# A hybrid trunk layer: convolution taps paced behind weight splits, and RWKV's GroupNorm as a step of its own

## The chip, the cores and the metric

One Trainium2 chip, one of its cores. The metric is the device time of one execution of the program in microseconds (us); the time of a kernel is the median of its runs.

## What is computed

One layer of a decoder trunk on x of 1024 tokens x 1024 channels, all in float32. One input projection feeds three groups of heads, and one output projection joins them; a gated MLP with a short convolution and a last norm follow.

```python
h = rms_norm(x, norm_mix)
p_conv, p_nsa, p_rwkv = split(h @ w_in)
y_conv = silu(layer_norm(causal_dwconv(u * sigmoid(gate), width 31)))   # 256 channels
y_nsa  = gates . (compressed, selected, sliding-window attention)       # 8 heads of 64
y_rwkv = (layer_norm_per_head(delta_rule_scan(r, w, k, v, a)) + bonus) * g   # 4 heads of 64
x = x + concat(y_conv, y_nsa, y_rwkv) @ w_out
x = x + (silu(causal_dwconv(h2 @ w_gate, width 3)) * (h2 @ w_up)) @ w_down    # h2 = rms_norm(x)
out = rms_norm(x)
```

`layer_norm_per_head` is the "GroupNorm" of this document: each head's 64 values are centred and scaled by the root of their variance, for each token.

## The kernel before

The program has phases. **Phase 1** makes all projections of the normalised input (the projection matmuls are L229), the convolution, and most of the RWKV group. **Phase 2** is the attention, one tile of 128 tokens after another (queries times keys L897/L898, transposes L922, probabilities times values L930), with the rest of the RWKV group between. Then come the output projection (**phase o**: loads of the joined groups L988, matmuls L229 into bank rw) and the MLP.

A projection block (`proj_T`) loads a weight block of 1024 x 128 in two halves (`wload`). Each half is split (`split`, L118) into a high part, copied and rounded by ACT (whi, L120), and a low part, the difference, made by DVE (wlo, L121). Then 24 matmuls of 512 columns for each half of the tokens follow (`mm3`, L229: high x high, high x low, low x high). PE reads the split parts, so ACT and DVE must split in time. Weights have two buffers (wraw, whi, wlo).

The convolution of width 31 works on 256 channels, as two tiles of 128 channels x 1024 tokens. Tile 0 is done by DVE: 31 instructions ("taps", L270 and 30 times L272) that multiply and add in place on 128 x 1024. Tile 1 is shared out: ACT scales a copy (ctap, L278) and POOL adds it (L279), 60 times on 128 x 512, and ctap has two buffers, so ACT can be two ahead of POOL. When both tiles are done, a LayerNorm over the channels follows (L284 on; its squares are L289, its matmuls L294 and L303). Its output goes to the DRAM tensor md (L311).

The RWKV group is worked off in four units (j, h): j picks two heads, h half of the tokens. A unit has three steps. S (`rwkv_prep`, `rwkv_mats`) prepares and, on POOL, runs a recurrence of 62 small instructions (L532, L534); its inputs and outputs go through DRAM. V (`rwkv_solve`) solves triangular systems with small matmuls (L554 to L581). C (`rwkv_chain`) runs over 8 chunks, each reading the state H that the one before has left (L597 to L615), and fills the PSUM bank py. In C, right behind the chunks, stands the GroupNorm (L619 to L642): sums and squares (L621 to L629), an inverse root on DVE (`rsqrt`, L106 to L116), four transposes on PE (L635), ACT's scale and shift (L637), the bonus and the gate (L638 to L641, with matmul L640), and a store to md (L642).

The order is made in two stages. The string `steps` gives the order in which the program's steps are written; RWKV's steps S, V and C are written under a high priority. Then a scheduler at build time lists every engine's instructions from these priorities and its own model of times. Each engine works its list strictly in order: an instruction that waits holds all behind it. SP issues all DMAs from one list in the same way. So a change of the steps moves instructions on all engines, far from where it was written. `hT` are the normalised inputs, `KEY.ev` below is the pair that evacuates a key projection: ACT's copy L689 and DVE's difference L690.

Before, the steps read

```python
steps="lora r0 S00 conv taps V00 S01 keys q C00 V01 r1a cmp0 r1b cmp1 r1c S10 C01 V10 S11 C10 V11 C11"
```

where keys, q, r1a, r1b, r1c, cmp0 and cmp1 are projections (keys, queries, the second pair of RWKV heads, compressed keys and values).

## Time and profile before

| | |
|---|---|
| median of 3 runs | 1483.7 us (1480.32 to 1494.8) |
| the profiled execution: its own time | 1479.4 us |
| its span (first to last instruction) | 1477.5 us |
| PE busy | 1388.7 us (94%) |
| DVE, ACT, POOL busy | 1002.7 (68%), 686.9 (46%), 499.2 (34%) us |
| share of PE in the chain that ended last | 79% |

PE is the engine that sets the time. It is idle for 89 us of the span, and those 89 us are not spread evenly: they lie around 165 to 245 us, around 361 to 377 us, and around 704 to 726 us. So the profile is read by stretches, and within each by what PE waited for. The granted clock of PE (PEclk, a share of full speed; the two levels are 1.2 and 2.4 GHz, so 0.50 is a stretch wholly at the lower one) is read beside it, because it has fallen wherever PE has been idle.

### The profile page before, as it was taken

To read this page: it belongs to the slowest core of one execution; us is meant where nothing else is said; L and a number is where in the kernel's file an instruction comes from. 1 tells how busy PE (TensorE), PEld (TensorE's weight loads), DVE (VectorE), ACT (ScalarE), POOL (GpSimd) and SP (SyncE) were. 2 spreads that over 40 slices of the span, in tenths; PEclk is the share of its full clock that TensorE was granted. 3 is DMA by queue.
4 is the path that set the end of the run, shared out by engine and by line. 5 is a ranking of instruction groups with operands and counts; after the bars stand their busy time and mean duration, and the time that the engine had idled before them with its cause. 6 is when DMAs were issued, how large, how long until landed. Compare 5 with 4: busy or idle time off the path is not lost.

```text
span 1477.5 us, 22767 instructions
## 1 busy us (share of the span) xinstructions
PE 1388.7 (94%) x7897; PEld 1095.2 (74%) x7897; DVE 1002.7 (68%) x2187; ACT 686.9 (46%) x1377; POOL 499.2 (34%) x607
## 2 busy tenths in 40 slices
PE   6999589998899999999799899999999999999997
PEld 5887457776677676766588677888788788888886
DVE  6347594454868778798257867676775776666685
ACT  5441245624456665678223533343343333445463
POOL 1002996921144066220000144443444442113310
PEclk9999888999899999999899999999999999999999
DMA  6133133436514254542722123332332334986533
GB/s 185 40 107 82 44 103 111 142 84 179 153 33 139 78 154 125 181 150 81 240 89 83 43 93 93 108 107 70 104 113 93 108 100 162 388 280 216 188 92 114
DMA packets 206679, 186.69 MB, mean 126 GB/s; under 512 B 56355, under 2 KB 145764, under 8 KB 206564
## 3 DMA queue, kind: packets, MB, share of 16 engines
q1 hardware_dynamic: 206564, 185.24, 40.3%
q8 instruction: 62, 1.02, 0.3%
q14 instruction: 53, 0.43, 0.1%
HBM read 126.99 MB, written 58.20 MB: 125 GB/s over the span
## 4 chain that ended last, share of the span: by engine, by line
PE 79%; DVE 8%; POOL 4%; DMA 3%; ACT 2%; issue 2%; SPq 1%; ACTq 0%; DVEq 0%; POOLq 0%
PE gb L229 13%; PE mm L229 12%; PE rw L229 10%; PE ga L229 9%; PE gc L229 8%; PE tr L229 5%; PE tr L922 5%; PE av L930 4%; PE mm L897 2%; PE mm L898 2%; POOL sT L534 1%; POOL sx L532 1%; DVE pp L901 1%; POOL cacc L279 1%; DVE pp L915 1%
## 5 line engine op out<-in xcount | busy, mean ns | idle before, releaser
L229 PE MATMUL mm<-hT,whi 128*128 128x512 f32 x608 | 200.3, 409 | 19.6 <-DVE ev L690 14.8
L229 PEld LDWEIGHTS mm<-hT,whi 128*128 128x128 f32 x608 | 115.7, 193 | 48.9 <-ACT whi L120 20.2
L229 PE MATMUL mm<-hT,wlo 128*128 128x512 f32 x304 | 123.0, 407 | 1.9 <-DVE wlo L121 1.9
L925 ACT ACTIVATE pT<-tr 128x512 f32<-128x512 f32 (+1 forms) x152 | 79.9, 536 | 60.6 <-PE tr L922 59.2
L930 PE MATMUL av<-pT,V 128*64 128x128 f32 x1056 | 96.0, 287 | 1.5 <-ACT pT L925 1.5
L1076 POOL TENSOR_TENSOR S<-wraw,wr 128x512 f32<-128x512 f32 x22 | 28.5, 1296 | 192.8 <-DVE or L107 91.1
L922 PE MATMUL tr<-idn,pp 128*128 128x128 f32 x528 | 90.3, 289 | 1.8 <-DVE pp L915 1.8
L279 POOL TENSOR_TENSOR cacc<-cacc,ctap 128x512 f32<-128x512 f32 x60 | 85.1, 1429 | 12.7 <-ACT ctap L278 12.4
L121 DVE TENSOR_TENSOR sp<-rb,sp 128x512 fp32r<-128x512 f32 x66 | 55.6, 842 | 49.4 <-ACT sp L120 49.4
L229 PE MATMUL rw<-woh,mix 128*128 128x512 f32 x240 | 79.5, 407 | 9.0 <-ACT mix L120 9.0
L229 PE MATMUL rw<-sp,sp 128*128 128x512 f32 x330 | 86.0, 389 | 0.0
L229 PE MATMUL tr<-sp,sp 128*128 128x512 f32 x330 | 85.9, 389 | 0.0
L897 PE MATMUL mm<-KH,QS 128*128 128x512 f32 (+2 forms) x192 | 77.7, 411 | 3.1 <-DVE mx L901 2.8
L930 PEld LDWEIGHTS av<-pT,V 128*64 128x64 f32 x1056 | 59.2, 136 | 28.3 <-issue 13.7
L922 PEld LDWEIGHTS tr<-idn,pp 128*128 128x128 f32 x528 | 55.9, 141 | 30.5 <-issue 29.1
L915 DVE TENSOR_SCALAR pp<-pp,sm 128x640 f32<-128x640 f32 (+7 forms) x128 | 76.5, 638 | 0.9
L120 ACT ACTIVATE sp<-rb 128x512 fp32r<-128x512 f32 x66 | 41.6, 630 | 74.1 <-PE tr L229 36.5
L121 DVE TENSOR_TENSOR sp<-b,sp 128x512 fp32r<-128x512 f32 x88 | 72.1, 827 | 5.2 <-ACT sp L120 5.0
L229 PEld LDWEIGHTS mm<-hT,wlo 128*128 128x128 f32 x304 | 58.5, 193 | 18.1 <-DVE wlo L121 3.8
L229 PEld LDWEIGHTS tr<-sp,sp 128*128 128x128 f32 x330 | 61.9, 188 | 12.9
L229 PEld LDWEIGHTS rw<-sp,sp 128*128 128x128 f32 x330 | 61.9, 188 | 12.9
L532 POOL TENSOR_TENSOR sx<-sN,sT 128x60 f32<-128x60 f32 (+24 forms) x124 | 48.0, 387 | 63.0 <-DMA sN<-dn 54.9
(455 smaller groups left out, 3648.8 us busy)
## 6 DMA issues: line engine op xcount, KB each, us to landing
wr<-in_ffn_w_gate_dram SPq DMA_DIRECT2D x44, 256.0 KB
wraw<-in_ffn_w_up_dram SPq DMA_DIRECT2D x44, 256.0 KB
pdS<-prod SPq DMA_DIRECT2D x44, 256.0 KB
b<-pdS SPq DMA_DIRECT2D x44, 256.0 KB
rb<-tdT SPq DMA_DIRECT2D x44, 256.0 KB
pdA<-prod SPq DMA_DIRECT2D x33, 256.0 KB
b<-pdA SPq DMA_DIRECT2D x33, 256.0 KB
wraw<-in_w_in_dram SPq DMA_DIRECT2D x30, 256.0 KB
```

Of the source, the lines that this page charges most:

```text
L120: self.nc.scalar.activation(hi, src, AF.Copy)
L121: getattr(self.nc, eng).tensor_tensor(lo, src, hi.bitcast(F32), op=ALU.subtract)
L229: mm = lambda l, r, **k: self.nc.tensor.matmul(out, l, r, skip_group_check=more, **k)
L279: nc.gpsimd.tensor_tensor(t[:, o:o + 512], t[:, o:o + 512], z, op=ALU.add)
L532: v_.tensor_tensor(x, N[:, q, q + 1:32].unsqueeze(2).to_broadcast([P, n, w]), Tm[:, q, 0:w].unsqueeze(1).to_broadcast([P, n, w]), op=ALU.mult)
L897: pe.matmul(pts[g][:, 0:n], QS[:, r, g, :], KH[g][hf][:, ks], start=True, stop=False)
L898: pe.matmul(pts[g][:, 0:n], QS[:, r, g, :], KL[g][hf][:, ks], start=False, stop=True)
L915: v.tensor_scalar(Ps[g], Ps[g], sm[:, g:g + 1], None, op0=ALU.mult)
L922: pe.transpose(pt[:, o:o + P], Ps[g][:, kt * P:kt * P + P], self.idn)
L925: s.activation(pT[:, 0:n], pt[:, 0:n], AF.Copy)
L930: pe.matmul(av[g * 64:g * 64 + 64, r * P:r * P + P], self.V[kk // 2][:, kk % 2, vo + g * 64:vo + g * 64 + 64], pT[:, o:o + P], start=first ...
L1076: gp.tensor_tensor(t, x, y, op=op)
```

## The change

Two things. First, the convolution is cut in two steps. `taps` (`conv_taps`) now writes the part of ACT and POOL at once, and puts the 31 instructions of DVE in a list, `self.fill`; each split of a weight half in `wload` then issues two of them (`pace=2`) behind itself. What is left, and the LayerNorm, is the new step `cend` (`conv_rest`), behind cmp0. Second, the GroupNorm is cut out of `rwkv_chain` and becomes `rwkv_norm`, a step N under the same high priority, that stands behind the next unit's solve (N11 behind C11). The work of every instruction stays what it was.

```diff
-steps="lora r0 S00 conv taps V00 S01 keys q C00 V01 r1a cmp0 r1b cmp1 r1c S10 C01 V10 S11 C10 V11 C11"
+steps="lora r0 S00 conv taps V00 S01 keys q C00 V01 N00 r1a cmp0 cend r1b cmp1 r1c S10 C01 V10 N01 S11 C10 V11 N10 C11 N11"
     def split(self, hi, lo, src, eng="vector"):
         self.nc.scalar.activation(hi, src, AF.Copy)
-        getattr(self.nc, eng).tensor_tensor(lo, src, hi.bitcast(F32), op=ALU.subtract)
+        return getattr(self.nc, eng).tensor_tensor(lo, src, hi.bitcast(F32), op=ALU.subtract).ins
...
-            self.split(hi, lo, raw)
+            ins = self.split(hi, lo, raw)
+            if self.fill:
+                with self.tc.issue_after(ins):
+                    for f in self.fill[:self.B["pace"]]:
+                        f()
+                    del self.fill[:self.B["pace"]]
...
+    def conv_taps(self):
+        nc = self.nc
+        self.cacc = [self.t4(name="cacc")[:, 0:T] for _ in range(2)]
+        def dve(d):
+            y, t, w = self.cy[0], self.cacc[0], self.cw[:, 0, d:d + 1]
+            if d == 0:
+                nc.vector.tensor_scalar(t, y[:, 0:T], w, self.cb[:, 0:1], op0=ALU.mult, op1=ALU.add)
+            else:
+                nc.vector.scalar_tensor_tensor(t, y[:, d:d + T], w, t, op0=ALU.mult, op1=ALU.add)
+        self.fill = [lambda d=d: dve(d) for d in range(31)]
+        y, t = self.cy[1], self.cacc[1]
+        for d in range(31):
+...
     def conv_rest(self):
         nc = self.nc
-        acc = [self.t4(name="cacc")[:, 0:T] for _ in range(2)]
-        for j in range(2):
-...
+        for f in self.fill:
+            f()
+        self.fill = []
+        acc = self.cacc
         for half in range(2):
 ...
         self.H = H
-
+        u.py = py
+
+    def rwkv_norm(self, u):
+        nc = self.nc
+        v, s, pe = nc.vector, nc.scalar, nc.tensor
+        j, py = u.j, u.py
         y3 = lambda t: t.rearrange("p (a b) -> p a b", b=64)
         m = self.small([P, 8], "gm1")
 ...
+        def norm(j, h):
+            with self.tc.high_priority(offset=100000):
+                self.rwkv_norm(us[j, h])
```

Line numbers of the changed kernel are larger: L272 becomes L277, L229 L235, L690 L712, L443 L459, L579 L595, L575 L591, L635 L657, L640 L662, L642 L664, L843 L865, L930 L952, L922 L944, L988 L1010.

In the cut parts of the diff the taps of tile 1 (POOL's first tap, then 60 pairs of ctap and add), the LayerNorm and the GroupNorm are what they were. On ACT, KEY.ev's copy L689 stands behind four ctaps before, and behind five after; the last two ctaps stand just ahead of the evacuation of r1a's second half in both.

**DVE, around the first key projections.** L272/L277 is a tap, L114 to L116 are steps of S01's inverse root, L121 a low part of weights, L690/L712 the difference of KEY.ev. Before:

```order
L114 TENSOR_TENSOR rs_t_397_2044<-rrn_2043 128x8
L272 SCALAR_TENSOR_TENSOR cacc_1581<-cy_1383,par,cacc_1581 128x1024
L115 TENSOR_TENSOR rs_t_397_2044<-rs_t_397_2044,rs_h_398_2047 128x8
L690 TENSOR_TENSOR ev_2278<-mm_430_2252,ev_2277 128x512
L272 SCALAR_TENSOR_TENSOR cacc_1581<-cy_1383,par,cacc_1581 128x1024
L116 SCALAR_TENSOR_TENSOR rrn_2043<-rs_t_397_2044,rrn_2043 128x8
L121 TENSOR_TENSOR wlo_2317<-wraw_2314,whi_2316 128x512
L272 SCALAR_TENSOR_TENSOR cacc_1581<-cy_1383,par,cacc_1581 128x1024
```

In the changed kernel:

```order
L115 TENSOR_TENSOR rs_t_369_1901<-rs_t_369_1901,rs_h_370_1904 128x8
L116 SCALAR_TENSOR_TENSOR rrn_1900<-rs_t_369_1901,rrn_1900 128x8
L459 COPY cum_1883<-rrn_1900 128x512
L712 TENSOR_TENSOR ev_2139<-mm_402_2113,ev_2138 128x512
L121 TENSOR_TENSOR wlo_2178<-wraw_2175,whi_2177 128x512
L277 SCALAR_TENSOR_TENSOR cacc_1581<-cy_1383,par,cacc_1581 128x1024 x2
L463 TENSOR_TENSOR lw_1876<-lw_1876,pm_1916 128x512
L466 TENSOR_SCALAR cum_1883<-tha_1880,par,r_ka_720 128x512
L121 TENSOR_TENSOR wlo_2186<-wraw_2183,whi_2185 128x512
L712 TENSOR_TENSOR ev_2170<-mm_405_2144,ev_2169 128x512
L277 SCALAR_TENSOR_TENSOR cacc_1581<-cy_1383,par,cacc_1581 128x1024
```

Before, 21 taps stand ahead of the first L690, and single taps stand between the steps of the inverse root. After, four stand ahead of the first L712, the inverse root runs through, and the other 27 are spread behind later splits.

**PE, from the last projection matmul of phase 1 to the first of the attention** (L229/L235 is the projection, L567 to L579 or L583 to L595 V01's solve, L415 to L446 or L431 to L462 the next unit's preparation, L843/L865 the first attention matmul). Before:

```order
L229 MATMUL mm_613_3361<-hT_107,wlo_3327 128x512
L579 MATMUL rw_2909<-W_2898,sN 64x64 x8
L575 MATMUL rw_2921<-VA_2137,GA_2098 64x64 x4
L575 MATMUL rw_2921<-VA_2152,GA_2098 64x64 x4
L579 MATMUL rw_2931<-W_2920,sN 64x64 x8
L415 MATMUL rw_3402<-lora_771,lw_w 128x512
L419 MATMUL rw_3406<-lora_771,lw_w 128x512
L437 MATMUL rw_3421<-bones,cum_3411 128x2 x4
L446 MATMUL rw_3444<-idn,cum_3411 128x128 x4
L843 MATMUL mm_4522<-kcmp_4433,q_816_4515 128x128 x4
```

In the changed kernel (thirteen small rows of the solve and of the LayerNorm stand between L235 and these):

```order
L595 MATMUL rw_2774<-W_2763,sN 64x64 x8
L319 MATMUL tr_566_3116<-cdg_3111,ones 128x512
L772 MATMUL tr_597_3292<-KC_3212,w_587_3213 128x130 x8
L657 MATMUL rw_2811<-idn,gyc_2788 128x128 x4
L662 MATMUL rw_2819<-lora_771,lw_w 128x512
L431 MATMUL rw_3402<-lora_771,lw_w 128x512
L788 MATMUL tr_601_3312<-w2v,hx_3210 128x64
L435 MATMUL rw_3406<-lora_771,lw_w 128x512
L865 MATMUL mm_4522<-kcmp_4433,q_816_4515 128x128 x4
L919 MATMUL mm_4542<-KH_4487,QS_4517 128x256
L920 MATMUL mm_4542<-KL_4493,QS_4517 128x256
L453 MATMUL rw_3421<-bones,cum_3411 128x2 x4
```

The GroupNorm of the first unit (L657, L662), which lay among projections, now stands behind the last of them and ahead of the first attention matmul, while the preparation's two last pieces (L453, and further down L462) now stand among attention matmuls. On SP the store of that GroupNorm (L664) now stands right ahead of the first load of queries.

**PE, the end of the attention** (L922/L944 and L930/L952 are attention, L631 of the changed kernel is the last unit's chain). Before:

```order
L930 MATMUL av_7701<-pT_7763,V_4513 64x128 x4
L922 MATMUL tr_7814<-idn,pp_7799 128x128 x4
L635 MATMUL rw_4413<-idn,gyc_4390 128x128 x4
L640 MATMUL rw_4421<-lora_772,lw_w 128x512
L930 MATMUL av_7701<-pT_7791,V_4513 64x128 x4
L930 MATMUL av_7701<-pT_7819,V_4513 64x128 x4
L866 MATMUL tr_7825<-idn,cmp_7702 32x128 x4
```

In the changed kernel:

```order
L952 MATMUL av_7701<-pT_7883,V_4513 64x128 x4
L944 MATMUL tr_7934<-idn,pp_7919 128x128 x4
L631 MATMUL rw_4303<-VA_3991,GR_3938 64x64
L631 MATMUL rw_4303<-VA_3991,GR_3939 64x64
L952 MATMUL av_7701<-pT_7911,V_4513 64x128 x4
L952 MATMUL av_7701<-pT_7939,V_4513 64x128 x4
L657 MATMUL rw_4413<-idn,gyc_4390 128x128 x4
L662 MATMUL rw_4421<-lora_772,lw_w 128x512
L235 MATMUL rw_8110<-woh_7950,mix_8096 128x512
```

Before, twelve rows of attention still followed the last GroupNorm's matmuls; now none does, and the last chain matmul (L631) is two rows from the attention's end. On SP, eight loads of x for the output tiles (xn, L992) used to stand ahead of the third load of mix (L988); in the changed kernel they stand ahead of the last GroupNorm's store and so ahead of all loads of mix.

## Rows read from the trace of the kernel before

**Rows 1.** The page: part 1, and part 5's group of the adds (mean in ns).

```profile
PE 1388.7 (94%) x7897; PEld 1095.2 (74%) x7897; DVE 1002.7 (68%) x2187; ACT 686.9 (46%) x1377; POOL 499.2 (34%) x607
...
L279 POOL TENSOR_TENSOR cacc<-cacc,ctap 128x512 f32<-128x512 f32 x60 | 85.1, 1429 | 12.7 <-ACT ctap L278 12.4
```

**Rows 2.** PE by stretches: from:to, us, PE busy (instructions), granted clock, DMA share, GB/s.

```profile
128.00:165.75 37.75, 37.75 (x183) 1.00 0.32 74
180.85:245.00 64.15, 53.09 (x302) 0.78 0.35 99
245.00:291.70 46.70, 46.70 (x250) 1.00 0.46 142
361.00:377.00 16.00, 8.47 (x65) 0.65 0.82 253
```

**Rows 3.** Waits of PE from 160 to 260: us in total, times, longest.

```profile
PE mm L229 <- DVE ev L690: 14.8, 1, 14.8
PE pm L478 <- DVE cum L476: 4.9, 1, 4.9
```

**Rows 4.** Waits of ACT from 128 to 260, and of POOL from 174 to 292.

```profile
ACT ctap L278 <- POOL cacc L279: 41.6, 22, 19.2
...
POOL cacc L279 <- ACT ctap L278: 12.4, 8, 4.4
```

**Rows 5.** POOL in two stretches of S00's recurrence, columns as in rows 2.

```profile
139.00:164.00 25.00, 22.96 (x25) 1.00 0.33 75
164.00:174.00 10.00, 8.12 (x26) 0.86 0.00 0
```

**Rows 6.** DVE's taps alone (L272) in two stretches, columns as in rows 2.

```profile
139.00:164.00 25.00, 18.83 (x15) 1.00 0.33 75
...
180.00:212.00 32.00, 20.74 (x10) 0.76 0.31 85
```

**Rows 7.** POOL from the end of that recurrence to the last add, columns as in rows 2.

```profile
174.00:212.00 38.00, 37.86 (x34) 0.72 0.26 71
212.00:292.00 80.00, 65.97 (x68) 0.91 0.43 128
```

**Rows 8.** PE between the phases, in order of time: start, us, instruction [idle before].

```profile
360.48 0.40 PE L229 MATMUL mm<-hT,wlo 128*128 128x512 f32 x1
...
369.92 1.86 PE L437 MATMUL rw<-bones,cum 128*128 128x2 f32 x8 [3.02 <-ACT cum L434]
...
376.73 0.55 PE L843 MATMUL mm<-kcmp,q 128*128 128x128 f32 x1 [0.82 <-DMA q<-qd]
```

**Rows 9.** SP, the first load of queries, in order of time.

```profile
372.69 0.57 SPq L830 DMA_DIRECT2D q<-qd  x1
```

**Rows 10.** DVE, first and last instruction of the first GroupNorm ahead of PE's L635.

```profile
327.76 0.69 DVE L621 TENSOR_REDUCE gm<-rw 128x8 f32<-128x512 f32 x1
...
333.89 0.69 DVE L632 TENSOR_TENSOR gyc<-gyc,gr 128x512 f32<-128x512 f32 x1
```

**Rows 11.** The last GroupNorm and the output projection, PE and SP, in order of time.

```profile
693.63 0.60 PE L635 MATMUL rw<-idn,gyc 128*128 128x128 f32 x4
694.16 1.12 PE L640 MATMUL rw<-lora,lw_w 64*128 64x512 f32 x2
...
697.10 0.34 SPq L642 DMA_DIRECT2D md<-gz  x1
...
701.23 0.43 SPq L988 DMA_DIRECT2D mix<-md  x1
...
715.36 0.38 SPq L988 DMA_DIRECT2D mix<-md  x1
...
706.95 0.71 PE L229 MATMUL rw<-woh,mix 128*128 128x512 f32 x1 [3.19 <-ACT mix L120]
...
725.87 0.79 PE L229 MATMUL rw<-woh,mix 128*128 128x512 f32 x1 [5.81 <-ACT mix L120]
```

**Rows 12.** PE behind the output projection's second wait, columns as in rows 2.

```profile
725.87:730.60 4.73, 4.73 (x11) 0.50 0.30 91
```

More of the change, by code (lines that the diff above doesn't have):

```diff
@@ L23, in __init__ @@
         self.B = dict(b2=20, wraw=2, whi=2, wlo=2, t4=4, rraw=2, cy=2, hx=12, ev=3, cv=2, lora=2, rb=20, at=2, pr=7, rt=2,
[L24 to L25 removed]
+                      QS=2, pp=6, q8=2, pT=5, pace=2, xn=8, ds=((), (0, 1, 2), (3, 4), (5, 6, 7), (8, 9), (10,), (), ()), h2=14, graw=2, prod=5, ft=4, u=4, wr2=4, wfh=3, wfl=3, S=2, p1=2, om=6, grow=2, pre=2, ap=(), wf=("own", "wf", "om"), hd=("vector",) * 4, tq=((0, 1, 2, 3),), ttag=("tr", "rw"),
+                      mm=3, tr=2, av=1, rw=2, mm1=2, tr1=2, pm=2, early="00 01", ga=2, gb=1, gc=1, y=16, r4=15, ta=3, tb=4, mid=2, de=dict(S3="gpsimd", T3="vector", T1="gpsimd", T2="gpsimd", T4="vector", S1="gpsimd", S2="gpsimd", S4="gpsimd"), order=(7, 6, 5, 4, 0, 3, 2, 1), sc=0, pk=1280, st="sync", last=5, sub="gpsimd",  steps="lora r0 S00 conv taps V00 S01 keys q C00 V01 N00 r1a cmp0 cend r1b cmp1 r1c S10 C01 V10 N01 S11 C10 V11 N10 C11 N11", both=0, cm="gpsimd", rpu=(), wo="vector", tap=(0, 31), vt="cv", vs="vector", va={1: (0, 1), 3: (2, 3), 5: (4, 5), 7: (6, 7)}, vq="sync", vl=1, vw=1, t1=("pm", "tr1"), into={6: (6, 2), 4: (4, 2), 3: (3, 1), 2: (2, 1), 1: (1, 1), 0: (0, 1)})
         self.B.update(bufs or {})
@@ L259, in conv_proj @@
             self.cy.append(y)
+    def conv_taps(self):
[10 more added lines that the diff above has]
+        for d in range(31):
+            w = self.cw[:, 1, d:d + 1]
+            if d == 0:
+                nc.gpsimd.tensor_scalar(t, y[:, 0:T], w, self.cb[:, 1:2], op0=ALU.mult, op1=ALU.add)
+            else:
+                for o in (0, 512):
+                    z = self.xt([P, 512], "cv", name="ctap")
+                    nc.scalar.activation(z, y[:, o + d:o + d + 512], AF.Copy, scale=w)
+                    nc.gpsimd.tensor_tensor(t[:, o:o + 512], t[:, o:o + 512], z, op=ALU.add)
     def conv_rest(self):
         nc = self.nc
[L263 to L279 removed]
+        for f in self.fill:
+            f()
+        self.fill = []
+        acc = self.cacc
         for half in range(2):
@@ L1322, in build @@
         for st in self.B["steps"].split():
-            if st[0] in "SVC" and len(st) == 3:
-                dict(S=start, V=solve, C=chain)[st[0]](int(st[1]), int(st[2]))
+            if st[0] in "SVCN" and len(st) == 3:
+                dict(S=start, V=solve, C=chain, N=norm)[st[0]](int(st[1]), int(st[2]))
             else:
```

20 lines of the change are left out of this document (2 added, 18 removed).

## The prediction

> **What bounds the kernel now.** I read the busy shares first: PE works 1388.7 us of the span [rows 1], so a change gains only by removing PE's idle time or its slow clock, and loses only by adding some. The table by stretches says where the idle time is. PE is full and at granted clock 1.00 up to 165.75. It stands until 180.85. From there to 245 it has 53.1 us of work in 64.2, at 0.78. From 245 to 291.7 it is full again, and between the phases 8.5 us of work lie in 16 [rows 2].
>
> The list of waits says why. The first stop is 14.8 us, for DVE's half of KEY.ev (L690), and a later one of 4.9 us is for S01's preparation on DVE [rows 3]. But DVE is not the cause of the first. Its L690 waits for ACT's copy L689, which stands in ACT's list behind four ctaps, and ACT has waited 19.2 us in one piece for POOL to free a ctap buffer [rows 4]. POOL was still at S00's recurrence, and that is late because of the taps: beside 15 of them, 25 instructions of POOL took 25 us; with no tap beside, 26 took 10 us [rows 5, 6]. So POOL's pace is 0.385 us an instruction when it has its way, and a tap takes (25 - 25 x 0.385)/15 = 1.03 us from it. The cost runs the other way too: a tap takes 18.83/15 = 1.26 us beside the recurrence and 2.07 beside the adds [rows 6].
>
> **Part 1, the taps.** No instruction is added or removed; 31 taps move. Ahead of the first L690 stood 21 of them, now four.
>
> Without taps beside it, S00's 51 instructions from 139 take 51 x 0.385 = 19.6 us and end at 158.6, not near 174. The first adds follow at 1.43 us each [rows 1], and ACT's copy, which needs about four of them done, comes near 165.5, when PE asks for it. Four taps and the inverse root then stand ahead of L712 on DVE. I put the stop at 2 us instead of 14.8, so PE is ahead by 13 us at this point.
>
> Can it keep that? The last two ctaps stand ahead of r1a's second evacuation on ACT, in both lists, so PE cannot get past r1a before POOL's last add, now at 291.7. POOL took 118 us from 174 to there, of which 12.4 were waits for ACT [rows 4, 7], and ten taps beside it cost 10 x 1.03 = 10.3. The work itself is 118 - 12.4 - 10.3 = 95.3 us. After the change all 31 taps lie beside it: 95.3 + 31 x 1.03 = 127.2 us, from 158.6 to 285.8 without any wait, and to 298 with the old 12.4. Most of those waits arose while PE stood and ACT waited for it, so I take 2 us of them: 288, which is **-4 us** for the stretch, between -8 (some taps cost POOL less) and +6. The 15 us saved on the recurrence are given back to the same lock between DVE and POOL, only later.
>
> The Trainium skill has a rule for this pair ("SBUF — State Buffer", section "Who interferes with whom"): a DVE instruction with two inputs in SBUF, as a tap is, contends with a GpSimd instruction that reads SBUF; whoever issues first holds the shared ports for its whole instruction and the other fully blocks. It speaks against this change, since moving taps from one POOL loop to another moves the blocking with them. The trace nearly agrees: a tap of 1.26 us takes 1.03 from POOL. By the rule as written, a tap would cost POOL its whole 1.26: 118 - 12.4 - 12.6 + 31 x 1.26 = 132 us, the last add at 290.7, and the stretch would give -1 instead of -4.
>
> **Part 2, the first GroupNorm, between the phases.** Now the last projection matmul starts at 360.48 and ends at 360.9, and the first attention matmul starts at 376.73, 15.8 us later [rows 8]; with a wait of 3.0 us for S10's preparation in between, and it ends on the query load, issued at 372.69 and so 4.0 us in flight [rows 8, 9]. After the change the GroupNorm of unit 00, covered by projections before, stands in this gap, and its store stands ahead of the query load on SP. The chain behind the last projection: the rest of V01's solve and of the LayerNorm until the GroupNorm's squares can run, 2.5 to 8 us (I take 6, as ACT has the solve's copies first); L621 to the end of L632, 333.89 + 0.69 - 327.76 = 6.8 [rows 10]; from L635 to the store 697.10 - 693.63 = 3.5 [rows 11]; the wait of SP and the queries' issue about 1.4; their landing 4.0. Together 21.7, against 15.8. What was done ahead of the last projection and now lies in the gap is taken off: L635 and L640, 1.7 [rows 11], and LayerNorm and compressor matmuls, which I estimate at 2.7 from their count beside L640's 1.12 for two of 512 columns. S10's last pieces, L453 and L462, now run among attention: at full clock some 1.2 back. 21.7 - 15.8 - 4.4 + 1.2 = **+3 us**, between -2 (the GroupNorm starts early) and +7 (all of it waits for the LayerNorm).
>
> **Part 3, inside the attention.** Units 01, 10 and 11 come later, among more attention matmuls. The GroupNorms of 01 and 10 still lie among PE work that does not need them, so I cost them at nothing; a GroupNorm without cover costs 6.8 + 3.5 [rows 10, 11]. The chain's matmuls are in PE's list and hold it when DVE is late: **+1 us**, between -3 and +5.
>
> **Part 4, the last GroupNorm.** This is the largest cost. Before, its L635 starts at 693.63, the store is issued at 697.10, the first load of mix at 701.23, and the first output matmul starts at 706.95 after 3.19 us of idle, so attention ends at 703.76 [rows 11]. After, the last chain matmul stands two rows from the attention's end, near 702.5. Then: 6.8 for L621 to L632, 0.5 to start L635 (709.8), 3.5 to the store (713.3), its landing, which the mix load needs, and which I put at 3.3 (by the query load 4.0, below nothing known), then 5.7 from issue to matmul (706.95 - 701.23): 722.3. The output starts 15.4 us later. Back come the second wait of 5.81 [rows 11], since the third mix load no longer stands behind the eight xn loads, and the slow clock behind it: 4.73 us at 0.50 [rows 12], 2.4 us of loss. The longer idle ahead of the output costs such a slow stretch in turn, about 1.6 more than now; and the GroupNorm's 1.7 us of PE work is no longer inside the attention but under this wait. 15.4 - 5.8 - 2.4 + 1.6 - 1.7 = 7.1; the chain steps squeezed into the last attention rows may stop PE for 1 to 4. I take **+8 us**, between +2 (the second wait goes, the landing is short) and +15 (the second wait stays).
>
> **The sum**, against the profiled execution's own 1479.4 us: -4 + 3 + 1 + 8 = +8, 1487. The median of the runs shown is 4.3 us above that execution; a run of the changed kernel at the same offset would read 1492.
>
> **Rivals.** *PE keeps what it gains* (faster). If a tap costs POOL 0.38 us or less, not 1.03, the adds end by 158.6 + 95.3 + 31 x 0.38 = 265.7, and PE gets back all idle time to 245: 14.8 + 64.15 - 53.09 = 25.9 us, with parts of the slow clock left over. 1479.4 - 26 + 12 = 1465. For it: in the stretch to 292 POOL still waited 12.4 us, so it is not full [rows 4]. Against: what a tap takes there, 1.03 us [rows 5]. Chance 0.20.
>
> *The wait changes its name* (no change or a little slower). The weights' low parts wait on DVE behind pairs of taps at 2.07 us, 4.1 us in each 5.0 us of projection half (24 matmuls at 37.75/183 = 0.21 [rows 2]), and PE waits for wlo instead of KEY.ev. Then the stretch gives +5: 1496. For it: taps at 2.07 us [rows 6]. Against: weights have two buffers, so each split has the time of a half block to be late in. Chance 0.10.
>
> *The last chain runs out of cover* (slower). If the last L631 falls behind the attention's end, the whole of chain end, GroupNorm, store and load is open: 20 us and more, and with a second wait of 5.81 kept and parts 1 to 3 at -1, +3, +3 the time is 1479.4 + 5 + 20 = 1504. It decides from the point where the chain's last chunk is ready later than 703.8. For it: only two rows stand between now. Chance 0.27.
>
> **How the numbers follow.** My forecast, the two effects nearly cancelling with the end of the attention the larger: chance 0.43, alone 1475 to 1499. Measurement of this kernel can tell about 1% from no change, 15 us, so faster means below 1469 and slower above 1498. Faster is the first rival, 0.20; same is my forecast with the second, 0.53; slower is the third, 0.27. Half of the first and a good part of the third are left out by 1463 to 1505.
>
> **What would show it.** In the changed profile: the wait for KEY.ev falls below 5 us; S00's recurrence ends near 159; the last add lies between 284 and 298, and PE waits there for ACT's evacuation or for wlo; taps have a mean near 2 us. Between the phases the first attention matmul comes 20 us or more behind the last projection, released by the query load. The output's first matmul waits 15 us or more for mix, and the 5.8 us wait is gone. If the last add comes before 270, part 1 is wrong, and the time is nearer 1465; if the output matmul waits under 8 us, part 4 is.

## The result, and the profile after

The changed kernel takes 1496.7 us (median of 18 runs, 1493.3 to 1502.0) where the kernel before takes 1482.3 in as many runs (1480.3 to 1494.8). The ratio is 1.0089, 95% interval 1.0073 to 1.0105 (the two medians alone give 1.0098): some 13 us slower and clear of the noise, but inside the 1% that the prediction counted as the same, and inside its range. The profiled execution has a span of 1492.8 us against 1477.5.

The span is split at three places that every kernel here has: the first attention matmul, the attention's end, the first output matmul. All times come from the timelines of the two profiled executions.

| stretch | before | after | difference |
|---|---|---|---|
| start to first attention matmul | 376.7 | 373.2 | -3.5 |
| first attention matmul to the attention's end (703.8, 705.9) | 327.0 | 332.7 | +5.7 |
| attention's end to first output matmul (707.0, 730.8) | 3.2 | 24.9 | +21.7 |
| from there to the end of the span | 770.5 | 762.0 | -8.5 |

The three places named ahead of the change hold 42 us of the 89 us that PE stood before: 25.8 from 165 to 245, 7.5 from 361 to 377, 8.8 from 704 to 726. The rest lies mostly at the program's start (15.5 up to 60), inside the attention (9.9), and behind 726, so the change cannot gain the whole 89.

**The convolution.** PE by stretches in the kernel after (columns as in rows 2), and the waits of PE there:

```profile
128.00:166.90 38.90, 38.89 (x190) 1.00 0.31 72
166.90:172.10 5.20, 0.00 (x0) 0.99 0.00 0
172.10:245.00 72.90, 65.42 (x406) 0.93 0.42 116
245.00:288.30 43.30, 35.84 (x148) 0.88 0.36 116
```

```profile
PE mm L235 <- DVE ev L712: 6.9, 2, 5.2
PE mm L235 <- DVE wlo L121: 5.6, 6, 2.8
PE mm L235 <- ACT q L840: 2.9, 1, 2.9
```

The one stop of 14.8 us [rows 3] has become a stop of 5.2 and eleven small ones, and the stretch after 172 is better filled than it was, 65.4 of 72.9 us against 53.1 of 64.2 [rows 2]. But PE, full from 245 on before, now has 7.5 us of holes between 245 and 288.3. That is where POOL is still adding. POOL's stretches, and ACT's longest group of waits:

```profile
139.00:164.00 25.00, 21.17 (x49) 1.00 0.34 75
164.00:212.00 48.00, 47.20 (x41) 0.89 0.33 90
212.00:288.00 76.00, 73.41 (x62) 0.93 0.39 119
```

```profile
ACT ctap L287 <- POOL cacc L288: 61.0, 43, 9.9
```

S00's recurrence does 49 instructions in the 25 us that gave it 25 [rows 5], and the first add comes at 164.6 instead of 174.9. Then POOL is full to the last add at 288.3 (291.7 before). Of the 10 us won at the head, 3.4 are left at the tail.

**The gap between the phases.** PE, in order of time:

```profile
365.19 0.66 PE L657 MATMUL rw<-idn,gyc 128*128 128x128 f32 x4 [1.73 <-DVE gyc L654]
...
373.24 2.04 PE L865 MATMUL mm<-kcmp,q 128*128 128x128 f32 x8 [1.31 <-DMA q<-qd]
...
375.50 1.70 PE L453 MATMUL rw<-bones,cum 128*128 128x2 f32 x8
...
385.32 0.66 PE L462 MATMUL rw<-idn,cum 128*128 128x128 f32 x4
...
398.58 1.02 PE L494 MATMUL rw<-cum,bones 128*128 128x512 f32 x2
```

The attention starts 3.5 us earlier than in [rows 8], though the last projection ended 12 us earlier (348.8): the solve, the LayerNorm and the GroupNorm lie in between. The rows to look at are the other ones. L453, L462 and L494 are S10's preparation. Before, they ran at 369.9, 374.8 and 383.2 (the row follows), two of them ahead of any attention; now they are spread among attention matmuls, and the last of them starts 15 us later.

```profile
383.17 1.12 PE L478 MATMUL rw<-cum,bones 128*128 128x512 f32 x2 [0.58 <-DVE cum L476]
```

**S11's recurrence on POOL**, before and after, as whole stretches (columns as in rows 2):

```profile
539.30:564.90 25.60, 19.90 (x64) 1.00 0.36 100
```

```profile
566.30:609.00 42.70, 30.94 (x73) 1.00 0.53 165
```

It starts 27 us later and takes 43 us instead of 26: in this stretch POOL now also works off ten sums of down weights (L971 to L974, 1.3 us each, among its first steps), of which nine lay elsewhere before. That is 13 us; another 6.1 us POOL stands at 599.7 for a small attention step, ahead of the last steps of the recurrence.

**The end of the attention.** PE, then SP, in order of time:

```profile
712.98 1.12 PE L657 MATMUL rw<-idn,gyc 128*128 128x128 f32 x4 [7.03 <-DVE gyc L654]
...
730.80 0.79 PE L235 MATMUL rw<-woh,mix 128*128 128x512 f32 x1 [14.70 <-ACT mix L120]
```

```profile
716.99 0.50 SPq L664 DMA_DIRECT2D md<-gz  x1
718.07 5.78 SPq L993 DMA_DIRECT2D wraw<-in_w_out_dram  x3
723.89 1.06 SPq L1367 DMA_DIRECT2D grow<-in_norm_ffn_dram  x2
725.05 0.38 SPq L1010 DMA_DIRECT2D mix<-md  x1
```

The last GroupNorm's transposes come 19 us later than before (693.63 in [rows 11]). PE stands 7.0 us for them and 14.7 for what follows: the store at 717.0, the load of mix at 725.1 behind three loads of output weights and two of a norm's weights, and its landing. The second wait of 5.8 us [rows 11] is gone.

### The profile page after: what moved, and what is told of

The parts are those of the page before. It is cut to its first block, busy times and chain, and to the rows that moved or that the text cites. A ratio compares the mean times of both kernels' runs of the same rounds, so it can differ in the third digit from the quotient of the medians.

```text
span 1492.8 us, 22750 instructions
## 1 busy us (share of the span) xinstructions
PE 1398.3 (94%) x7897; PEld 1100.4 (74%) x7897; DVE 1008.1 (68%) x2187; ACT 687.9 (46%) x1377; POOL 505.9 (34%) x607
## 4 chain that ended last, share of the span: by engine, by line
PE 68%; DVE 9%; POOL 6%; DMA 3%; issue 2%; ACT 2%; SPq 1%; DVEq 0%; ACTq 0%
PE gb L235 12%; PE rw L235 11%; PE ga L235 9%; PE gc L235 8%; PE tr L235 5%; PE tr L944 4%; PE av L952 4%; POOL cacc L288 4%; PE mm L235 3%; PE mm L919 2%; PE mm L920 2%; POOL sT L550 1%; POOL sx L548 1%; DMA wraw<-in_w_out_dram 1%; DVE pp L937 1%
## 5 line engine op out<-in xcount | busy, mean ns | idle before, releaser
L235 PE MATMUL mm<-hT,whi 128*128 128x512 f32 x608 | 199.5, 410 | 12.3 <-DVE ev L712 6.9
L235 PEld LDWEIGHTS mm<-hT,whi 128*128 128x128 f32 x608 | 116.7, 195 | 42.0 <-ACT whi L120 10.7
L235 PE MATMUL mm<-hT,wlo 128*128 128x512 f32 x304 | 124.5, 413 | 5.6 <-DVE wlo L121 5.6
L952 PE MATMUL av<-pT,V 128*64 128x128 f32 x1056 | 94.9, 288 | 3.9 <-ACT pT L947 3.9
L288 POOL TENSOR_TENSOR cacc<-cacc,ctap 128x512 f32<-128x512 f32 x60 | 97.2, 1634 | 1.3 <-ACT ctap L287 1.2
L235 PE MATMUL rw<-woh,mix 128*128 128x512 f32 x240 | 77.7, 400 | 14.7 <-ACT mix L120 14.7
L121 DVE TENSOR_TENSOR sp<-rb,sp 128x512 fp32r<-128x512 f32 x66 | 56.8, 861 | 51.2 <-ACT sp L120 51.1
L944 PE MATMUL tr<-idn,pp 128*128 128x128 f32 x528 | 90.2, 290 | 0.1
L235 PE MATMUL rw<-sp,sp 128*128 128x512 f32 x330 | 86.0, 389 | 0.0
L235 PE MATMUL tr<-sp,sp 128*128 128x512 f32 x330 | 85.8, 389 | 0.0
L952 PEld LDWEIGHTS av<-pT,V 128*64 128x64 f32 x1056 | 59.0, 137 | 31.8 <-issue 14.0
L944 PEld LDWEIGHTS tr<-idn,pp 128*128 128x128 f32 x528 | 56.1, 141 | 29.2 <-issue 27.0
L121 DVE TENSOR_TENSOR wlo<-wraw,whi 128x512 fp32r<-128x512 f32 x55 | 48.7, 887 | 41.7 <-ACT whi L120 39.6
L235 PEld LDWEIGHTS mm<-hT,wlo 128*128 128x128 f32 x304 | 59.2, 195 | 23.4 <-DVE wlo L121 9.0
L937 DVE TENSOR_SCALAR pp<-pp,sm 128x640 f32<-128x640 f32 (+7 forms) x128 | 72.3, 605 | 1.0
L121 DVE TENSOR_TENSOR sp<-b,sp 128x512 fp32r<-128x512 f32 x88 | 68.8, 790 | 5.2 <-ACT sp L120 4.8
L287 ACT ACTIVATE ctap<-cy,par 128x512 f32<-128x512 f32 x60 | 43.2, 722 | 61.5 <-POOL cacc L288 61.0
```

The costliest lines, as they stand in the source:

```text
L121: return getattr(self.nc, eng).tensor_tensor(lo, src, hi.bitcast(F32), op=ALU.subtract).ins
L235: mm = lambda l, r, **k: self.nc.tensor.matmul(out, l, r, skip_group_check=more, **k)
L287: nc.scalar.activation(z, y[:, o + d:o + d + 512], AF.Copy, scale=w)
L288: nc.gpsimd.tensor_tensor(t[:, o:o + 512], t[:, o:o + 512], z, op=ALU.add)
L937: v.tensor_scalar(Ps[g], Ps[g], sm[:, g:g + 1], None, op0=ALU.mult)
L944: pe.transpose(pt[:, o:o + P], Ps[g][:, kt * P:kt * P + P], self.idn)
```

## Experiments

Every kernel but e12 has a ratio to the kernel before, which ran beside it on the same chip (its medians there were 1484.1 with e1 to e4, 1481.1 with e5 to e8, 1481.6 with e9 to e12), with a 95% interval. The table has the landmarks from each timeline; "S10 ready" is the start of the last matmul of S10's preparation (L478 in the kernel before), "last norm" the start of the last GroupNorm's transposes (L635). Line numbers in rows are those of the kernel that ran, a few lines apart from one kernel to the next.

| kernel | S10 ready | S11's recurrence | last norm | attention | first output | median | ratio |
|---|---|---|---|---|---|---|---|
| before | 383.2 | 539 to 565 | 693.6 | 376.7 to 703.8 | 707.0 | 1482.3 | 1 |
| after | 398.6 | 566 to 609 | 713.0 | 373.2 to 705.9 | 730.8 | 1496.7 | 1.0089 (1.0073 to 1.0105) |
| e1, taps alone | 391.9 | 562 to 604 | 711.8 | 374.3 to 720.9 | 726.5 | 1497.2 | 1.0086 (1.0044 to 1.0127) |
| e2, GroupNorm alone | 402.8 | 563 to 604 | 712.8 | 378.3 to 703.9 | 730.2 | 1494.8 | 1.0083 (1.0056 to 1.0110) |
| e3, only N00 deferred | 398.8 | 561 to 601 | 715.3 | 373.4 to 708.1 | 733.2 | 1496.9 | 1.0090 (1.0057 to 1.0124) |
| e4, after, xn late | 398.1 | 566 to 611 | 717.2 | 372.8 to 710.2 | 732.5 | 1494.3 | 1.0069 (1.0038 to 1.0101) |
| e5, e1 + S10's L462 first | 385.2 | 569 to 611 | 716.6 | 377.9 to 728.3 | 731.5 | 1500.0 | 1.0142 (1.0111 to 1.0173) |
| e6, after + S10's L462 first | 387.2 | 547 to 575 | 715.6 | 379.8 to 722.7 | 730.9 | 1496.9 | 1.0110 (1.0087 to 1.0133) |
| e7, before + delay in S10 | 418.5 | 570 to 615 | 711.6 | 377.9 to 710.6 | 726.9 | 1494.9 | 1.0086 (1.0063 to 1.0109) |
| e8, e1 + S10's L494 first | 383.0 | 544 to 568 | 699.2 | 384.8 to 711.0 | 713.3 | 1481.6 | 0.9986 (0.9960 to 1.0011) |
| e9, after + S10's L494 first | 386.8 | 550 to 580 | 717.9 | 388.7 to 725.0 | 732.4 | 1502.1 | 1.0132 (1.0084 to 1.0180) |
| e10, e8 + N00 behind S10 | 384.0 | 564 to 610 | 717.5 | 385.8 to 724.5 | 736.2 | 1505.6 | 1.0153 (1.0102 to 1.0204) |
| e11, e8 + xn late | 383.1 | 546 to 570 | 700.0 | 384.9 to 712.0 | 713.8 | 1476.5 | 0.9958 (0.9940 to 0.9976) |
| e12, after without 30 taps (convolution unfinished) | 372.6 | 544 to 585 | 700.4 | 357.3 to 694.7 | 719.6 | 1483.6 | one run |

### First: which part costs?

My first theory was the table of stretches read part by part: the taps win their 3.5 us, the deferred GroupNorms lose the rest. Four kernels tested it.

**e1, the taps alone.** The GroupNorm goes back into its chain.

```diff
-steps="... C00 V01 N00 r1a cmp0 cend r1b cmp1 r1c S10 C01 V10 N01 S11 C10 V11 N10 C11 N11"
+steps="... C00 V01 r1a cmp0 cend r1b cmp1 r1c S10 C01 V10 S11 C10 V11 C11"
         def chain(j, h):
                 self.rwkv_chain(us[j, h])
+                self.rwkv_norm(us[j, h])
```

> Part 1 alone: DVE's taps two behind each split, the GroupNorm back in the chain (steps V01 r1a cmp0 cend ... C11). Theory: the conv stretch gains the 3 to 5 us that the changed kernel shows (last add 288.3 for 291.7), and the 13 us at the end of attention and the 6 us inside it come from part 2, so this kernel ends 2 to 6 us below the kernel before (ratio about 0.997), with the last GroupNorm's L657 near 690. Rival (the taps' move itself shifts all RWKV units late): ratio 1.005 or more, L657 beyond 705.

Measured: 1497.2, as slow as both parts together, with the last norm at 711.8. My theory fell, the rival held. The conv stretch does gain what it should (last add 289.8, last projection 350.6 instead of 360.9, attention 2.4 us earlier), and yet the last norm is 18 us late, with no GroupNorm moved.

**e2, the GroupNorm alone.** All DVE taps are issued in one go, with the LayerNorm behind them.

```diff
-steps="... conv taps V00 ... r1a cmp0 cend r1b ..."
+steps="... conv taps cend V00 ... r1a cmp0 r1b ..."
-        self.fill = [lambda d=d: dve(d) for d in range(31)]
+        self.fill = []
+        for d in range(31):
+            dve(d)
```

> Part 2 alone: the GroupNorm as step N, the taps all at once as before. Theory: the stop for KEY.ev is 14 to 15 us again, the last unit's L657 comes 15 to 20 us later than in the kernel before and the output's first matmul 20 us or more, so the time is 12 to 20 us above the kernel before (ratio about 1.010). Rival (part 2 costs only together with the spread taps): ratio 1.000 to 1.003.

Measured: 1494.8; the attention's end is where it was, the last norm at 712.8 and the first output matmul at 730.2. The expectation held. So each part costs about 13 us alone, and both cost 13 together. Two causes that do not add up are either one and the same, or one hides the other; I took them for one, and the third part below shows that there are two.

**e3, only N00 deferred**, and **e4, the loads of x later**:

```diff
-... S10 C01 V10 N01 S11 C10 V11 N10 C11 N11
+... S10 C01 N01 V10 S11 C10 N10 V11 C11 N11
```

```diff
-            nc.sync.dma_start(mf, self.md[:, u * 4:u * 4 + 4, x])
+            ld = nc.sync.dma_start(mf, self.md[:, u * 4:u * 4 + 4, x]).ins
-        nc.sync.dma_start(xt, self.a["x"][0, x])
+        with self.tc.issue_after(ld):
+            nc.sync.dma_start(xt, self.a["x"][0, x])
```

> The changed kernel with steps N01 and N10 right behind their own chains again (C01 N01 V10, C10 N10 V11); only N00 stays deferred. Theory (the units of phase 2 are late because the bank py stays held through the next solve and the GroupNorm stands ahead of the next unit's preparation): most of the 19 us by which the last L657 came later goes away, the time falls to about the kernel before (1478 to 1485). Rival (the deferral of N00 into the gap between the phases is what delays all later units): within 3 us of the changed kernel, about 1492 to 1497.

> The changed kernel, but each load of x for an output tile is issued behind that tile's loads of mix, so that the eight no longer stand ahead of the last store of the GroupNorm. In the changed kernel that store was issued at 716.99 and the first load of mix only at 725.05, behind loads of output weights that had to wait. Theory (transfers in the way cost part of the end): the load of mix comes 4 us behind the store as in the kernel before, and 4 to 8 us are gained, 1485 to 1490. Rival (the late chain alone sets the end): within 2 us of the changed kernel.

Measured: 1496.9 and 1494.3. In e3 nothing is won by putting N01 and N10 back; its rival, that the delay is set between the phases, fits the time, though this run alone does not show it. In e4 the load of mix stood 4.7 us behind the store, as expected, but the store itself was at 722.5; the intervals of e4 and of the changed kernel overlap, so e4 tells nothing on the time.

### Second: the head of the RWKV chain

All four have in common that S10 is ready 9 to 20 us late. So I formed another theory. RWKV is one serial chain (S10, its recurrence, C01, V10, S11, C10, V11, C11, last norm, store, load of mix), and it is as long as the whole attention: before, it reached its last norm at 693.6, and PE already waited 3.2 us for mix behind the attention's end [rows 11]. A delay at its head would then be a delay of the output. And S10 is late because the new lists put the first attention rows ahead of its preparation, on PE (the rows above) and on DVE.

**e7, a delay at the head of the chain.** To the kernel before, latency is added in S10:

```diff
         tha = pr("tha")
         s.activation(tha, pa, AF.Tanh, scale=0.5, bias=self.a0h[:, js])
+        if (j, h) == (1, 0):
+            for _ in range(18):
+                s.activation(lw, lw, AF.Copy)
         v.tensor_scalar(lw, lw, c2, c2, op0=ALU.mult, op1=ALU.add)
```

> The kernel before, with 18 copies of 128x512 in place put into S10's preparation on ACT, some 11 us of added latency at the head of the RWKV chain and no other change. New theory: with taps and GroupNorm as before, the end of the attention goes the way of the changed kernel: last GroupNorm at 705 to 715, output's first matmul waits 10 us or more, time 1488 to 1498 (ratio 1.004 to 1.010). Rival (the chain had slack, and the changed kernel's loss is that of its taps and GroupNorm): 1480 to 1485.

Measured: 1494.9, ratio 1.0086. With taps and GroupNorm untouched, this kernel goes the way of the changed one: the same last norm (711.6), the same collision on POOL (570 to 615, with nine sums of down weights between). Its preparation is in PE's list as late as this:

```profile
377.87 2.05 PE L846 MATMUL mm<-kcmp,q 128*128 128x128 f32 x8 [10.03 <-DMA q<-qd]
387.62 1.70 PE L440 MATMUL rw<-bones,cum 128*128 128x2 f32 x8
406.12 0.60 PE L449 MATMUL rw<-idn,cum 128*128 128x128 f32 x4
418.52 1.02 PE L481 MATMUL rw<-cum,bones 128*128 128x512 f32 x2
```

An added 11 us made S10 35 us late, since attention rows moved in ahead of it; so this is not a pure delay, the build's lists changed with it. And then 17 us of those 35 were made up on the way: the chain is not without slack, it passes on a part of a delay at its head.

**e8 and e5, the taps alone, with S10 first.** The first attention tile is issued on PE behind a chosen matmul of S10: in e8 behind L494, the last of its preparation, in e5 behind L462, as the kernel before happens to have it.

```diff
+        if (j, h) == (1, 0):
+            self.s10 = ins          # e8: of pe.matmul(px, ...), e5: of the last pe.transpose(pb, ...)
...
         for n, i in enumerate(order):
-            self.attn_tile(i)
+            if n:
+                self.attn_tile(i)
+            else:
+                with self.tc.issue_after(self.s10):
+                    self.attn_tile(i)
```

> As the kernel with part 1 alone and S10 first, but the first attention tile waits in PE's list for the last matmul of S10's preparation, L494. New theory: attention starts 5 to 8 us later, the chain's head is 2 to 4 us earlier still; the attention then ends later by what it started later, 1472 to 1486. Rival as for that kernel: 1490 or more.

> Part 1 alone once more, and PE's first attention tile is issued behind S10's transposes L462, as the kernel before happens to have it. New theory: RWKV is one serial chain from S10 to the last GroupNorm, as long as the whole attention; with part 1 alone S10's L494 came at 391.9 for 383.2 and its store for the recurrence at 404.6 for 391.9, S11's recurrence then fell together with POOL's sums of down weights (41 us for 26), and the last GroupNorm came at 712 for 694. With S10 first: store by 392, S11's recurrence about 26 us long, last GroupNorm at 685 to 697, output's first matmul by 710, time 1468 to 1482 (ratio 0.990 to 1.000). Rival (the spread taps delay RWKV by other ways, or the scheduler's new order inside the attention): 1490 or more.

Measured: e8 at 1481.6, all the loss of e1 gone (0.9986 against 1.0086), by an order alone. The time is as expected, the way to it is not: the attention was to start 5 to 8 us later and to end later by as much. PE pays for it in the gap and gets it back at the end:

```profile
371.39 1.87 PE L453 MATMUL rw<-bones,cum 128*128 128x2 f32 x8 [2.48 <-ACT cum L450]
376.26 1.11 PE L462 MATMUL rw<-idn,cum 128*128 128x128 f32 x4 [3.00 <-DVE cum L459]
382.98 2.05 PE L494 MATMUL rw<-cum,bones 128*128 128x512 f32 x2 [5.61 <-DVE cum L492]
384.82 1.92 PE L867 MATMUL mm<-kcmp,q 128*128 128x128 f32 x8
```

```profile
PE rw L235 <- ACT mix L120: 5.9, 3, 3.3
```

The attention starts at 384.8 for e1's 374.3, and ends at 711.0 for 720.9. S11's recurrence takes 23 us, with no sum of down weights in it.

e5 missed, and its rival held: 1500.0. S10 was ready at 385.2, 7 us earlier than in e1, but V10 came at 489.6, later than e1's 482.0. Between them stands the GroupNorm of unit 01, whose small DVE instructions wait in DVE's list among those of the attention; it took from 455.2 to 482.8 in e5, and 14 us (445.0 to 459.7) in e8:

```profile
455.18 0.69 DVE L645 TENSOR_REDUCE gm<-rw 128x8 f32<-128x512 f32 x1 [0.18 <-PE rw L633]
...
482.13 0.69 DVE L656 TENSOR_TENSOR gyc<-gyc,gr 128x512 f32<-128x512 f32 x1
```

So the head is not all: with S10 only 2 us later than in e8, e5 is 18 us slower. Each step of the chain can lose its lead, and then S11's recurrence falls into POOL's sums (569 to 611 here). Which attention work the lists put between the steps is decided anew in each build, and I cannot say from these runs why e5's lists came out worse than e8's there. Nor was a change tried that should cost nothing, to see how far a new list alone moves the time. The nearest to it are e4 and e11, which alter only the place of late loads: their last norms stay within 4.2 and 0.8 us of those of the kernels they alter.

### Third: what the deferred GroupNorm costs when the head is right

**e6 and e9** are the changed kernel, whole, with the same two orders (e6 behind L462, e9 behind L494).

> The changed kernel with the first attention tile behind S10's L462 on PE. New theory: S10's store comes 10 us or more earlier than in the changed kernel (408.9) and the time falls by 8 to 18 us, to 1478 to 1488; the deferred GroupNorms keep a few us of cost against the taps alone. Rival (the place of the GroupNorm behind all attention matmuls is what costs): within 3 us of the changed kernel, 1493 to 1499.

> The changed kernel whole, with its first attention tile behind S10's last matmul of preparation (L494) on PE, so that it differs from the kernel with part 1 alone and the same order (1481.6) by the deferred GroupNorms alone. Theory: the head of the RWKV chain is mended, but the GroupNorm of unit 10 between V11 and C11 keeps the bank py and delays the last chain, as in the run with L462 first, where V11 came 3 us earlier than before and C11 28 us later: 1490 to 1498. Rival (with the head mended the deferral is free): 1478 to 1485.

Measured: 1496.9 and 1502.1. e6's expected gain did not come, and its rival's time held; e9 ended slower than expected, and its rival is out. e8 and e9 differ by the deferral alone, so with the head mended the deferred GroupNorms cost some 20 us (1.0132 against 0.9986). Which of the four costs it was not tried one by one; the trace points to N10: V11 starts at 601.7 in e9 and 613.2 in e8, so e9 is ahead; C11's first state comes at 651.3 in e9 and 633.9 in e8. Between lies N10. In e9 (DVE, then PE):

```profile
600.31 0.69 DVE L645 TENSOR_REDUCE gm<-rw 128x8 f32<-128x512 f32 x1
...
621.86 0.68 DVE L648 TENSOR_TENSOR gyc<-rw,gm 128x512 f32<-128x512 f32 x1
...
642.88 0.69 DVE L656 TENSOR_TENSOR gyc<-gyc,gr 128x512 f32<-128x512 f32 x1
```

```profile
615.14 1.14 PE L593 MATMUL rw<-VA,GA 64*64 64x64 f32 x16
618.60 1.14 PE L597 MATMUL rw<-W,sN 64*64 64x64 f32 x16
622.70 1.14 PE L593 MATMUL rw<-VA,GA 64*64 64x64 f32 x16
625.68 1.14 PE L597 MATMUL rw<-W,sN 64*64 64x64 f32 x16
644.02 1.06 PE L659 MATMUL rw<-idn,gyc 128*128 128x128 f32 x4
```

The GroupNorm that takes 6.8 us among projections [rows 10] takes 43 us here, from 600.3 to 643.6, since V11 and the attention stand between its instructions. All that time it holds the second bank of rw, or stands ahead of C11 in the order, and C11's first matmul comes only behind it, at 648.2. V11 itself runs with one bank, each matmul group waiting until the last was copied out (3.0 to 4.1 us apart); in e8 the groups of both head halves overlap. That one bank is the reason for the spacing is argued from `rw=2` in the code, not tried.

The changed kernel has this delay too. PE, the first matmul of V11 and of C11 before, then V11, N10 and C11 in the changed kernel:

```profile
601.32 1.19 PE L554 MATMUL rw<-DF,GA 32*32 32x32 f32 x32
...
617.49 0.43 PE L595 MATMUL rw<-rH,AT 128*64 128x128 f32 x2
```

```profile
616.95 1.19 PE L570 MATMUL rw<-DF,GA 32*32 32x32 f32 x32 [2.82 <-DMA DF<-dt]
...
658.47 0.60 PE L657 MATMUL rw<-idn,gyc 128*128 128x128 f32 x4
...
663.10 0.32 PE L611 MATMUL rw<-rH,AT 128*64 128x128 f32 x1
```

V11 waits for S11's result and comes 16 us late; N10 takes from 608.5 to 657.8 on DVE, and C11 is 46 us late. The end of the chain then makes up 26 of the 46, for the last norm is 19 us late. So two delays lie one behind the other, and the four kernels show why they do not add up: late head and deferral 1.0089 (after), late head alone 1.0086 (e1), deferral alone 1.0132 (e9), neither 0.9986 (e8). Only with both gone is the loss gone. e5 is the exception, with a head 2 us late, no deferral, and 1.0142.

**e10, N00 behind S10**, tried to use the earlier V01 of a deferred GroupNorm, on top of e8:

```diff
-... C00 V01 r1a cmp0 cend r1b cmp1 r1c S10 C01 V10 ...
+... C00 V01 r1a cmp0 cend r1b cmp1 r1c S10 N00 C01 V10 ...
```

> Part 1, S10's preparation ahead of the first attention tile, and of the GroupNorms only the first one deferred, behind S10 (V01 ... S10 N00 C01); the others in their chains. V01 can then start near 330 and S10's preparation near 352, for 346 and 364 with no deferral. Theory (the gap between the phases is S10's preparation behind V01 and N00): attention starts at 371 to 377 for 384.8, and the time is 1470 to 1478. Rival (with py00 held, solve and preparation share one bank and lose what they gain, or the preparation waits for its loads of r and k): 1480 to 1490.

Measured: 1505.6, the slowest of all. The preparation started at 358.7, 6 us earlier than in e8, but was ready at 384.0, 1 us later; PE then waited for it longer (3.9, 4.0 and 5.6 us). The rival's mechanism (the preparation loses what it gains) is in the rows, but the time lies far outside its range too. V10 was at 484.2, 18 us later than in e8, and the rest of the chain followed; why V10 came so late was not found.

### Fourth: the end, and the taps

**e11** puts the order of e4 (each x load behind its tile's loads of mix) on e8.

> The kernel with part 1 alone and S10's preparation first (1481.6), with each load of x for an output tile issued behind that tile's loads of mix. Theory: the third load of mix no longer stands behind eight transfers of 512 KB, and the output projection's waits shrink by 0 to 4 us: 1477 to 1482. Rival (these loads are then late for their addition): 1482 or more.

Measured: 1476.5, ratio 0.9958 (0.9940 to 0.9976): 0.4% faster than the kernel before, and by the ratios 1.3% faster than the changed one. The output's waits for mix fell to

```profile
PE rw L235 <- ACT mix L120: 2.3, 2, 1.9
```

That is 3.6 us less than in e8, of the 5 us between the two kernels' medians. The two ran on different chips, and their intervals overlap (0.9960 to 1.0011 for e8), so that this order by itself gains is likely, not shown.

**e12, no taps on DVE.** One tap of 31 is left, and the convolution's first channel tile is unfinished.

```diff
-        self.fill = [lambda d=d: dve(d) for d in range(31)]
+        self.fill = [lambda d=d: dve(d) for d in range(1)]
```

> The changed kernel without 30 of DVE's 31 taps, so the convolution's first channel tile is left unfinished. It measures what a tap takes from POOL. Theory (1.03 us of POOL for each tap, as in S00's recurrence): 25 to 30 taps less beside the adds, and the last add falls from 288.3 to 258 to 265. Rival (the adds wait for ACT and PE and the taps cost POOL nothing): 284 to 289.

Measured: the last add at 264.3, 24.0 us earlier. Over 30 taps that is 0.80 us each, and 0.92 over the 26 that in the changed kernel's trace start behind 164. But POOL was not full in e12. Its waits for a ctap, in e12 and then in the changed kernel:

```profile
POOL cacc L288 <- ACT ctap L287: 7.2, 11, 1.4
```

```profile
POOL cacc L288 <- ACT ctap L287: 1.2, 1, 1.2
```

So 6 us of what the taps had taken went into waiting. From the first add to the last, POOL needs 102.3 - 7.2 = 95.1 us without taps and 123.7 - 1.2 = 122.5 with 26 of them. That is 27.4 us, or 1.05 us a tap; five small steps of recurrences fewer lie in that stretch of e12, so it is about 1.0. The theory held, and its price of 1.03 too.

PE was full from 245 on, and the last projection ended at 332.2 instead of 348.8. The one run gave 1483.6 us: with the taps gone from DVE, and 16 us won in phase 1, the kernel is still no faster than the one before. S11's recurrence started at 544, as in e8, and yet took 41 us, with twelve sums of down weights in it; the last norm came at 700.4, the first output matmul at 719.6.

## Why the prediction was right, point by point

The direction came out, and the size was some 7 us short (1487 forecast, +8 of the profiled execution; +15 between the two profiled executions, +13 by the runs), and the range of 1463 to 1505 held. Not all of the steps did, and that the whole stayed near the middle of the range is in part luck: the loss inside the attention and at its end came from a chain that the prediction had costed at nothing.

- **Part 1, the taps: right in size and reason.** Forecast -4 us, last add at 288; measured last add 288.3, -3.4. That what is saved on the recurrence goes back to the same pair of engines is what e12 shows: a tap costs POOL about 1.0 us, where the sum had 1.03. And the 95.3 us that it had for POOL's work without taps and waits are 95.1 in e12. Some smaller numbers were off. The recurrence made room for the first add at 164.6, not at 158.6, since three taps and other DVE work still ran beside it: 10 us saved, not 15. So the stop for KEY.ev was 5.2 us and not 2, a little above the 5 us given as a sign. And a tap takes 1.8 us beside the adds (26 in 46.5 us from 164 to 289), not 2.07. Some waits did change their name, as the second rival had it: 5.6 us are now for wlo, and 2.9 for the queries' evacuation.
- **The rule of the Trainium skill** ("SBUF — State Buffer", "Who interferes with whom"), that one of the two blocks the other for a whole instruction, would have put the last add at 290.7; it came at 288.3. The trace nearly agrees with it: about 1.0 us taken from POOL by a tap that lasts 1.28 us when POOL stands (the rows are in the last section). The 1.8 us of a tap beside the adds hold its own waiting for POOL.
- **Part 2, the gap: forecast +3, measured 0.** The first attention matmul comes 24.5 us behind the last projection, released by the query load, as said. The chain was longer than the 21.7 us of the sum: L657 stood at 365.2, 16.4 us behind the last projection where the sum has 6 + 6.8, and the store 3.7 us behind that. But the work that moved into the gap was under-booked by more: 8.7 us and not 4.4, for the last projection ended 12.1 us earlier, the last add only 3.4. 24.5 - 15.8 - 8.7 = 0.
- **The step that failed** stands at the end of part 2: "S10's last pieces, L453 and L462, now run among attention: at full clock some 1.2 back". I booked at 1.2 us of PE's time what e7 and e8 show to be enough for the whole loss. And part 3 costed the later units at nothing because they "still lie among PE work that does not need them". PE does not need them, but the output does, and the chain that leads there passes delays on: I had its end in the rows (the first output matmul waiting 3.2 us for mix [rows 11]) and did not read it as the end of a chain that starts at S10. By e9, the deferral of those units costs some 20 us even when S10 is in time. Measured for the inside of the attention: +5.7, not +1; the rest of the delay shows at its end.
- **Part 4: the steps behind the last chain were right, 5 us short, and the cause was not the one I gave.** Forecast +8; measured 21.67 - 8.54 = +13.1. L657 at 713.0 (forecast 709.8), store 717.0 (713.3), output 730.8 (722.3); the second wait is gone as said. The output's wait for mix was 14.7 us, a little under the 15 given as a sign, behind 7.0 for the GroupNorm. The mis-sized term is the way from the store to the load of mix, 3.3 in the sum and 8.1 in the trace, behind output weights on SP; the sum was below the 4.1 us that its own rows have for this way (697.10 to 701.23 [rows 11]). The other 3.7 us of the 8.5 are the store's own delay. But I took the late chain as given by the order. It is not the step N11 that puts the GroupNorm behind the attention: in e1 no GroupNorm is moved, and its L657 is at 711.8.
- **The rivals.** The first (PE keeps its gain, 0.20) is out, and its price was wrong too: in e12 the last add comes at 264.3, ahead of the 265.7 that it asks for, and the time is 1483.6, not 1465. The second (the wait changes its name, 0.10) named 1496, near the result, but by a stretch of +5 that measured -3.5. The third (the last chain runs out of cover, 0.27, 1504) was nearest in kind: the last chain ended at 704.9, 1 us ahead of the attention's end, and 24.9 us followed until the output; but no second wait was left.

By terms the errors are +0.5, -3, +5 and +5 us, 7 us in all: the sum stayed in the range since each was small beside the range, and the gap's lay on the other side.

## What to carry to other kernels

When a scheduler at build time interleaves two streams, find the serial chain that runs through the stretch, and look whether something already waits for its end (here PE, for 3.2 us) before costing a shift at its head at nothing; a build may reorder that head for a change made 200 us away. Test it by a delay at the head of the chain (e7), then by pinning the head's order (e8): if the first reproduces the loss and the second removes it, the loss is the order's and not the work's. Here that clears the taps, in one order at least; the deferred GroupNorms cost time with the head in order too (e9). And when two parts each cost as much alone as both do together, do not take them for one cause before both have been taken away one by one and together. Work moved off one busy engine gains only what its neighbour on the shared path does not pay again; measure that by leaving the work out (e12), and count the waits that appear in its place.

## What the runs showed of the hardware

A tap of DVE (128 x 1024, both inputs in SBUF) and an instruction of POOL hardly run side by side here: the one that starts second is held for most of what is left of the first. In the kernel before, a tap takes 1.28 us while POOL has nothing to do (128.93). At 158.27 a tap starts just ahead of a step of the recurrence. The tap takes its 1.27 us, and the step 1.36, where a step of this kind takes 0.31 alone:

```profile
128.93 1.28 DVE L272 SCALAR_TENSOR_TENSOR cacc<-cy,par,cacc 128x1024 f32<-128x1024 f32 x1
...
158.27 1.27 DVE L272 SCALAR_TENSOR_TENSOR cacc<-cy,par,cacc 128x1024 f32<-128x1024 f32 x1
158.33 1.36 POOL L532 TENSOR_TENSOR sx<-sN,sT 128x63 f32<-128x63 f32 x1
...
163.96 0.31 POOL L532 TENSOR_TENSOR sx<-sN,sT 128x76 f32<-128x76 f32 x1
```

In the changed kernel an add is under way when a tap starts at 217.27. The tap waits for it and takes 2.30 us, and the next add waits for the tap and takes 2.27, where the shortest add takes 1.25:

```profile
217.27 2.30 DVE L277 SCALAR_TENSOR_TENSOR cacc<-cy,par,cacc 128x1024 f32<-128x1024 f32 x1
...
218.44 2.27 POOL L288 TENSOR_TENSOR cacc<-cacc,ctap 128x512 f32<-128x512 f32 x1
```

So a tap costs POOL about 1.0 us beside the adds (e12), and 1.03 by the estimate beside the small steps of the recurrence, as I had expected; and beside the adds it often waits for POOL in turn.
